# A hand-ordered opening of the first feed-forward stage, with kept normed tiles and another order of its first gate products

## The chip, the cores and the metric

The kernel runs on one core of a Trainium2 chip. The metric is the device time of one execution in microseconds (us), the median of several runs. The engines are PE (TensorE, matrix products), DVE (VectorE), ACT (ScalarE), POOL (GpSimd) and SP (SyncE, which here issues the loads and stores). PEld is the loading of weights into PE, beside PE's products.

## What is computed

The reference is a decoder layer of width 1024 over 1024 tokens with 16 meta tokens in front of them, 1040 columns in all. A gated feed-forward half step comes first, then two attention branches, then a second feed-forward half step and a last norm. Only the opening of the first feed-forward step is touched here:

```python
def rmsnorm(x, g):
    xf = x.astype(jnp.float32)
    y = xf * lax.rsqrt(jnp.mean(xf * xf, axis=-1, keepdims=True) + EPS)
    return (y * g.astype(jnp.float32)).astype(x.dtype)

def swiglu(x, w_gate, w_up, w_down):
    return (jax.nn.silu(x @ w_gate) * (x @ w_up)) @ w_down

h = h + 0.5 * swiglu(rmsnorm(h, norm_ffn1[l]), w_ffn1_gate[l], w_ffn1_up[l], w_ffn1_down[l])
```

The hidden width is 2816, that is 22 blocks of 128 columns.

## The kernel before

**Layout.** The activations lie transposed: eight tiles (k = 0 to 7) of 128 channels each, with the tokens as columns, in two halves x = 0 (528 columns, the meta tokens first) and x = 1 (512 columns). A product in float32 quality is made of three float16 products (`mm3`, lines 144 to 147): every weight and every activation is split into a high part, written by ACT, and the rest, written by DVE (here called the low part). A float32 weight piece of 128 x 1024 is loaded by SP (`load_raw`, line 126), its high part is made on L130 (ACT) and its low part on L131 (DVE).

**The norm of a half.** `square_into` (L157, L160, L161) squares each tile on ACT and adds up on DVE. For the second half POOL does both (L617, L619). `norm_stats` sums over the channels with PE (L171, one column for each block of 128 tokens), then takes the mean on DVE (L173), the root on ACT (L175), the reciprocal on DVE (L176), and makes one step of Newton's method in four small DVE instructions (L178 to L181). `norm_bcast` (L191) spreads the result over 128 partitions with PE, into PSUM. `norm_u` then makes for each k the normed tile "un" on DVE (L219, with the spread factor read from PSUM), its high part on ACT (L221) and its low part on DVE (L222). For the combined blocks below the spread factor is also kept in SBUF (rb, L224).

**The first pair.** `plain_pair(0)` (line 266) makes the first two gate blocks and the first two up blocks by plain products, one half and one piece of weights after the other (`proj`). The gate's result goes through Silu on ACT (L278), and is multiplied by the up result on DVE (L283). Between the halves the weights of the first combined job are made (`wide_weights`) and `make_t` is called.

**The combined jobs.** All other blocks go by a scheme of seven products in place of eight (a Strassen-like scheme over pairs of blocks). It needs four sums of activations t1 to t4. `make_t` computes the normed tiles a second time on DVE (`gained`, L302, from h, the gain and rb; four tiles that `norm_u` kept in `saved` are taken over), combines them on POOL (`combine`, L289 to L292, four subtractions for each of four i), and splits the results into "tb" tiles (`split_x`, L235 on ACT, L236 on DVE). `fast` (line 415) then emits the seven products (L327), one after the other, and after each of them lets `pump` emit a share of the side work that waits in `todo`: splits of hidden tiles (L540, L541), sums and splits of the next job's weights (L390 to L395, L341, L344). After that comes the reader of the product. Of the seven products p1 and c11 share the bank "pa": c11 adds onto p1, so c11 can only begin when ACT has copied p1 out ("base", L451). The order of a gate or up job is `UP` (line 434): p1, p6, p7, p5, c11, p74, p53. Here p6 reads t2, p7 reads t3, p5 reads t1, p74 reads t4, and p1, c11 and p53 read only plain activations.

**What sets the order.** In the combined jobs PE, DVE, ACT and POOL run exactly in the order in which the code emits their instructions (`tc.manual_schedule(engines=ORDERED)`, line 545); an instruction that waits holds up all that stand behind it on its engine. The opening, up to the end of `plain_pair`, is put in order by the framework's own scheduler. SP issues the loads in one queue: eight tiles of the first half, the unit matrix, the gains, two weight pieces, then eight tiles of the second half (L114); later pieces follow as buffers come free.

Of the kernel before, what the change touches and what calls it, by code (L numbers as in the profile page):

```python
# [9 lines left out]
F16 = mybir.dt.float16  # L10
# [4 lines left out]
ALU = mybir.AluOpType  # L15
# [40 lines left out]
def layer_kernel(ctx: ExitStack, tc: tile.TileContext, xT, gains, wgu1, wd1, win, wvi, wbs, wbw, wout,  # L56
# [52 lines left out]

    h = [[hp([P, HW[x]], F32, "h") for _ in range(KD)] for x in range(2)]  # L110

    def load_h(x):
        for k in range(KD):
            nc.sync.dma_start(h[x][k], xT[k][:, HS0[x]:HS0[x + 1]])  # L114

    load_h(0)
    ident = cst.tile([P, P], F32, name="ident")
    nc.sync.dma_start(ident, eye)
    g_all = cst.tile([P, 4, KD], F32, name="g_all")
# [43 lines left out]
    def new_acc():  # L163
        return big.tile([P, 528], F32, tag="acc", name="acc", bufs=2)

    def norm_stats(acc, subs):
        bl = blocks_of(subs)
        nb = len(bl)
        ps = trps("nsum")
        for j, (b0, _) in enumerate(bl):  # L170
            nc.tensor.matmul(ps[:, j:j + 1], acc[:, b0:b0 + P], ones, start=True, stop=True)  # L171
        a = small(8, "n_a")
        nc.vector.tensor_scalar(a[:, :nb], ps[:, :nb], 1.0 / D, EPS, op0=ALU.mult, op1=ALU.add)  # L173
        r = small(8, "n_r")
# [3 lines left out]
        nc.vector.tensor_mul(e[:, :nb], r[:, :nb], r[:, :nb])  # L178
        nc.vector.tensor_mul(e[:, :nb], e[:, :nb], a[:, :nb])
        nc.vector.tensor_scalar(e[:, :nb], e[:, :nb], -0.5, 1.5, op0=ALU.mult, op1=ALU.add)  # L180
        nc.vector.tensor_mul(r[:, :nb], r[:, :nb], e[:, :nb])  # L181
        return r

    def norm_bcast(r, subs):
        bl = blocks_of(subs)
# [41 lines left out]
    def ffn(u, rb, hs, gi, wgu, wd, other_half, passes, saved):  # L227
# [187 lines left out]
        def fast(weights, blocks, order):  # L415
            a11, a12, s2, s3, s1, s4, a22 = weights
            b11, b21, b22, t1, t2, t3, t4 = blocks
            what = {"p1": ("pa", a11, b11, wa, wa, True), "p6": ("pb", s2, t2, wa, wa, True),
                    "p7": ("pc", s3, t3, wb, wb, True), "p5": ("pd", s1, t1, wb, wb, True),
                    "c11": ("pa", a12, b21, wa, wa, False), "p74": ("pc", a22, t4, wa, wa, False),  # L420
                    "p53": ("pd", s4, b22, wb, wb, False)}
# [24 lines left out]
        def half_products(m, blocks, first, done):  # L446
            make = fbtmp if m else ftmp
            for what, ps in joint(blocks, UP):
# [3 lines left out]
                elif what == "p6":  # L452
                    nc.vector.tensor_add(va(base), ps, va(base))
                elif what == "c11":
                    first(ps)
                elif what == "p7":
                    c22 = make("c22")
                    nc.vector.tensor_add(vb(c22), ps, va(base)[:, :, :wb])  # L458
                elif what == "p5":
                    nc.vector.tensor_add(vb(c22), ps, vb(c22))  # L460
                    done(3, c22, vb(c22))
                elif what == "p74":
                    c21 = make("c21")
                    nc.vector.tensor_add(va(c21), ps, va(base))
                    done(2, c21, va(c21))
                else:
                    c12 = va(base)[:, :, :wb]
                    nc.vector.tensor_add(c12, ps, c12)
                    done(1, base, c12)

        def gate_part(blocks):
            gates = [None] * 4
# [70 lines left out]
        vals = plain_pair(0)  # L543
        blocks = (u[0][:4], u[0][4:], u[1][4:]) + tuple(t_blocks)
        with tc.manual_schedule(engines=ORDERED):
            for f0, f1 in F_GROUPS:
# [4 lines left out]
                for f in range(f0, f1, 2):  # L551
# [14 lines left out]
                        for i, t in ((0, spare), (2, vals[1]), (1, vals[0]), (3, vals[2])):  # L566
                            split_later(down[3 + i], t, i % 2 ^ 1, tail)
                    if f < NF - 2:
                        gates = gate_part(blocks)
# [27 lines left out]
            ready = acc, subs, done  # L597
        return acc

    u1, rb1 = [], []  # L600

    def ffn1_norm(x):
        acc = new_acc() if x == 0 else acc_b
        for k in range(KD if x == 0 else 0):
            square_into(k, h[x][k], acc)
        u, rb = norm_u(norm_stats(acc, SUB_ALL[x]), h[x], 0, SUB_ALL[x], keep=True, saved=saved1 if x else None)
        u1.append(u)
        rb1.append(rb)

    saved1 = {}  # L610
    raws = [load_raw(wgu1[i], 1024) for i in range(2)]
    load_h(1)
    ffn1_norm(0)
    acc_b = new_acc()
    for k in range(KD):
        sq = acc_b if k == 0 else ftmp("sq")
        nc.gpsimd.tensor_mul(sq[:, :512], h[1][k], h[1][k])  # L617
        if k:
            nc.gpsimd.tensor_add(acc_b[:, :512], acc_b[:, :512], sq[:, :512])  # L619
    u2 = []  # L620
    hsp = dram.tile([KD, P, T], F32, name="hspill")

    def mix_norm(x, r):
        u2.append(norm_u(r, h[x], 1, SUB_ALL[x]))
        for k in range(KD):
            nc.sync.dma_start(hsp[k][:, HS0[x]:HS0[x + 1]], h[x][k])

    acc = ffn(u1, rb1, h, 0, wgu1, wd1, lambda: ffn1_norm(1),
              ((0, SUB_ALL[0], lambda r: mix_norm(0, r)), (1, SUB_ALL[1], None)), saved1)
    close_phase()  # L630
    open_phase("mix")

# [569 lines left out]
```

## Time and profile before

| what | value |
|---|---|
| median of 3 runs | 2032.15 us (2031.77 to 2035.65) |
| profiled execution, its time | 2033.16 us |
| span of that execution in the profile | 2031.1 us |
| mean granted clock of PE, as a share of full speed | 0.988 |
| PE busy over the span | 1936.5 us, 95% |
| DVE busy over the span | 1627.2 us, 80% |
| ACT, POOL busy over the span | 901.0 us, 44%; 386.9 us, 19% |

The profile is of one execution: its own time lies 2.1 us above its span, and 1.0 us above the median. All stretches below are in microseconds from the span's start.

### The profile page before, as it was taken

To read this page: it belongs to the slowest core of one execution; us is meant where nothing else is said; L and a number is where in the kernel's file an instruction comes from. 1 tells how busy PE (TensorE), PEld (TensorE's weight loads), DVE (VectorE), ACT (ScalarE), POOL (GpSimd) and SP (SyncE) were. 2 spreads that over 40 slices of the span, in tenths; PEclk is the share of its full clock that TensorE was granted. 3 is DMA by queue.
4 is the path that set the end of the run, shared out by engine and by line. 5 is a ranking of instruction groups with operands and counts; after the bars stand their busy time and mean duration, and the time that the engine had idled before them with its cause. 6 is when DMAs were issued, how large, how long until landed. Compare 5 with 4: busy or idle time off the path is not lost.

```text
span 2031.1 us, 32839 instructions
## 1 busy us (share of the span) xinstructions
PE 1936.5 (95%) x13080; PEld 1197.3 (59%) x13080; DVE 1627.2 (80%) x2779; ACT 901.0 (44%) x1602; POOL 386.9 (19%) x313
## 2 busy tenths in 40 slices
PE   5899999999999989899999999998899999999997
PEld 4588888888888556454545654444344444444443
DVE  7888788778875799999999964566987787788767
ACT  4433233333323446589885643433433243233232
POOL 3611312221310132221001000002322212312200
PEclk9999999999999999999999999999999999999998
DMA  4011111111113543212020024241112121111213
GB/s 158 11 63 48 58 63 50 55 64 58 48 63 105 183 141 112 99 59 73 17 63 17 27 68 156 78 164 49 34 55 68 48 72 47 63 62 47 76 38 130
DMA packets 58873, 146.95 MB, mean 72 GB/s; under 512 B 7264, under 2 KB 13408, under 8 KB 58720
## 3 DMA queue, kind: packets, MB, share of 16 engines
q1 hardware_dynamic: 58720, 144.86, 22.3%
q8 instruction: 102, 1.67, 0.3%
q14 instruction: 51, 0.42, 0.1%
HBM read 130.01 MB, written 14.76 MB: 71 GB/s over the span
## 4 chain that ended last, share of the span: by engine, by line
PE 70%; DVE 18%; ACT 4%; issue 4%; DMA 2%; POOL 2%; DVEq 0%; SPq 0%; ACTq 0%; POOLq 0%
PE pc L327 14%; PE pd L327 14%; PE pa L327 14%; PE pb L327 7%; PE p_br L999 2%; DVE sc L791 2%; DVE u L222 2%; DVE wsp L131 1%; PE p_gate L147 1%; PE p_gate L145 1%; PE p_gate L146 1%; DVE m L790 1%; PE p_out L146 1%; PE p_out L147 1%; PE p_out L145 1%
## 5 line engine op out<-in xcount | busy, mean ns | idle before, releaser
L327 PEld LDWEIGHTS <-wsp 128*128 128x128 f16 x4176 | 410.0, 98 | 214.2 <-issue 12.3
L327 PEld LDWEIGHTS <-x 128*128 128x128 f16 x3132 | 307.3, 98 | 157.9 <-issue 8.5
L327 PE MATMUL pa<-u,wsp 128*128 128x264 f16 (+1 forms) x1440 | 224.7, 310 | 0.0
L131 DVE SCALAR_TENSOR_TENSOR wsp<-wst,wsp 128x1024 f16<-128x1024 f32 (+2 forms) x130 | 134.8, 1038 | 54.6 <-ACT wsp L130 54.3
L130 ACT ACTIVATE wsp<-wst 128x1024 f16<-128x1024 f32 (+2 forms) x130 | 111.7, 863 | 140.1 <-PE p_out L147 45.9
L147 PEld LDWEIGHTS <-wsp 128*128 128x128 f16 x912 | 90.5, 99 | 94.5 <-issue 12.3
L145 PEld LDWEIGHTS <-wsp 128*128 128x128 f16 x912 | 91.0, 100 | 85.1 <-issue 4.1
L146 PEld LDWEIGHTS <-wsp 128*128 128x128 f16 x912 | 90.7, 99 | 80.2 <-issue 3.9
L327 PE MATMUL pb<-tb,wsp 128*128 128x264 f16 (+1 forms) x720 | 113.7, 312 | 8.1 <-ACT tb L235 5.5
L327 PE MATMUL pc<-tb,x 128*128 128x264 f16 (+1 forms) x720 | 113.9, 313 | 6.6 <-DVE c L458 6.4
L327 PE MATMUL pc<-tb,wsp 128*128 128x256 f16 (+1 forms) x720 | 114.2, 314 | 0.0
L327 PE MATMUL pd<-tb,x 128*128 128x256 f16 (+1 forms) x720 | 110.7, 308 | 0.0
L327 PE MATMUL pd<-u,x 128*128 128x256 f16 (+1 forms) x720 | 110.7, 308 | 0.0
L289 POOL TENSOR_TENSOR t<-g,g 128x512 f32<-128x512 f32 x16 | 25.5, 1595 | 436.0 <-DVE g L494 436.0
L812 ACT ACTIVATE jk<-sc,s5nb 128x784 f16<-128x784 f32 (+2 forms) x93 | 97.9, 1052 | 19.0 <-DVE s5nb L827 15.3
L341 ACT ACTIVATE wsp<-sa 128x1024 f16<-128x1024 f32 (+1 forms) x62 | 60.2, 971 | 103.4 <-DVE sa L393 103.4
L327 PE MATMUL pa<-hid,wsp 128*128 128x264 f16 (+1 forms) x648 | 103.1, 310 | 0.0
L341 ACT ACTIVATE wsp<-wst 128x1024 f16<-128x1024 f32 (+1 forms) x62 | 59.9, 967 | 94.3 <-DMA wst<-in_wgu_dram 49.9
L327 PE MATMUL pd<-hid,x 128*128 128x256 f16 (+1 forms) x648 | 101.6, 308 | 0.0
L147 PE MATMUL p_gate<-u,wsp 128*128 128x512 f16 x256 | 97.0, 379 | 1.4 <-DVE wsp L131 1.4
L145 PE MATMUL p_gate<-u,wsp 128*128 128x512 f16 x256 | 97.0, 379 | 0.0
L146 PE MATMUL p_gate<-u,wsp 128*128 128x512 f16 x256 | 97.0, 379 | 0.0
(234 smaller groups left out, 4147.6 us busy)
## 6 DMA issues: line engine op xcount, KB each, us to landing
wst<-in_wgu_dram SPq DMA_DIRECT2D x88, 512.0 KB, 3.7
wst<-in_win_dram SPq DMA_DIRECT2D x44, 512.0 KB, 3.5
wst<-in_wd_dram SPq DMA_DIRECT2D x48, 384.0 KB, 3.4
wst<-in_wd_dram SPq DMA_DIRECT2D x32, 256.0 KB, 2.7
wst<-in_wout_dram SPq DMA_DIRECT2D x16, 512.0 KB, 4.1
qscr<-ry SPq DMA_DIRECT2D x20, 256.0 KB, 2.1
q<-qscr SPq DMA_DIRECT2D x20, 256.0 KB, 3.0
wst<-in_wbs_dram SPq DMA_DIRECT2D x16, 256.0 KB, 2.7
```

What stands on the lines that cost most here:

```text
L130: nc.scalar.activation(sp[:, 0, :n], st[:, :n], AF.Copy, scale=WS)
L131: nc.vector.scalar_tensor_tensor(sp[:, 1, :n], st[:, :n], WS, sp[:, 0, :n], op0=ALU.mult, op1=ALU.subtract)
L145: nc.tensor.matmul(ps, w[:, 0, wcols], xt[:, 0, xcols], start=start, stop=False)
L146: nc.tensor.matmul(ps, w[:, 0, wcols], xt[:, 1, xcols], start=False, stop=False)
L147: nc.tensor.matmul(ps, w[:, 1, wcols], xt[:, 0, xcols], start=False, stop=stop)
L222: nc.vector.tensor_sub(u[k][:, 1, s0:s1], t[:, :w], u[k][:, 0, s0:s1])
L289: nc.gpsimd.tensor_sub(vb(t1), vb(b1), va(a1)[:, :, :wb])
L327: nc.tensor.matmul(ps[:, s, :n], w[:, a, wc], tiles[k][:, y, s * stride:s * stride + n], start=start and k == 0 and j == 0, stop=stop and ...
L341: nc.scalar.activation(sp[:, 0, :n], st[:, :n], AF.Copy, scale=WS)
L791: nc.vector.match_replace(out=raw, in_to_replace=m8, in_values=raw, imm_value=MARK)
L812: nc.scalar.activation(junk[:, :w], sc[b][0], AF.Sign, bias=bias[:, j:j + 1], accum_out=s[:, j:j + 1])
L999: nc.tensor.matmul(pb, bw[:, a, c * P:(c + 1) * P], oT[:, y, c, :], start=c == 0 and n == 0, stop=c == 3 and n == 2)
```

## The change

The loads of the first half are cut at column 272: first eight loads of 272 columns, then the unit matrix, the gains and weight pieces 0, 1 and 2, then eight loads of the other 256 columns, then piece 3, then the second half. The pieces 2 and 3 go to other buffers ("wS"), so that they need not wait for the first two.

`first_pair` takes the place of `plain_pair(0)`, of the two norms before it, of `wide_weights` and of `make_t`, in the first stage alone. It handles the tokens in three slices (272, 256 and 512 columns), and its instructions on PE, DVE, ACT and POOL run in the order written. For each slice and each k the three steps "un", high, low are emitted one behind the other, and then the products of that k with the four weight pieces. The eight "un" tiles of each half are kept in full, and POOL combines these; nothing is computed twice. The squares of all slices are on ACT and DVE. The first slice's spread factor is read from PSUM, those of the other two are first copied to SBUF by ACT. The first gate job runs in the order `FIRST`, where c12 is made from a seventh product p3 = s4 b22 in a bank of its own in place of p53 added onto p5. Newton's step takes three DVE instructions in place of four in every norm of the kernel. The second feed-forward step keeps `plain_pair` and `gate_part`.

```diff
-    load_h(0)
+    CUT = 272
+    for k in range(KD):
+        nc.sync.dma_start(h[0][k][:, :CUT], xT[k][:, :CUT])
...
+    def newton(r, e, a):
+        nc.vector.scalar_tensor_tensor(e, r, -0.5, r, op0=ALU.mult, op1=ALU.mult)
+        nc.vector.tensor_mul(e, e, a)
+        nc.vector.scalar_tensor_tensor(r, e, 1.5, r, op0=ALU.add, op1=ALU.mult)
...
+                    "p53": ("pd", s4, b22, wb, wb, False), "p3": ("pb", s4, b22, wb, wb, True)}
...
+        def first_products(m, blocks, first, done):
+            for what, ps in joint(blocks, FIRST):
+                if what == "p1":
+                    base = fbtmp("base")
+                    nc.scalar.activation(va(base), ps, AF.Copy)
+                elif what == "p3":
+                    c12 = ftmp("c12")
+                    nc.scalar.activation(vb(c12), ps, AF.Copy)
+                elif what == "c11":
+                    first(ps)
+                elif what == "p7":
+                    c22 = ftmp("c22")
+                    nc.vector.tensor_add(vb(c22), ps, va(base)[:, :, :wb])
+                elif what == "p5":
+                    nc.vector.tensor_add(vb(c22), ps, vb(c22))
+                    nc.vector.tensor_add(vb(c12), ps, vb(c12))
+                elif what == "p6":
+                    nc.vector.tensor_add(vb(c22), ps[:, :, :wb], vb(c22))
+                    done(3, c22, vb(c22))
+                    nc.vector.tensor_add(va(base), ps, va(base))
+                    nc.vector.tensor_add(vb(c12), va(base)[:, :, :wb], vb(c12))
+                    done(1, c12, vb(c12))
+                else:
+                    c21 = ftmp("c21")
+                    nc.vector.tensor_add(va(c21), ps, va(base))
+                    done(2, c21, va(c21))
...
+            for k in range(KD):
+                sq(0, k)
+                if k:
+                    add(0, k)
+            stats(0, W[0][:, 1, :])
+            whi(0)
+            root(0)
+            rb[0] = spread(0, W[1][:, 1, :], False)
+            un_(0, 0), uhi(0, 0), ulo(0, 0)
+            wlo(0), whi(1)
+            mm(0, 0, 0)
...
+            stats(1, W[0][:, 1, :])
+            un_(0, 7), uhi(0, 7), ulo(0, 7)
+            root(1)
+            for i in range(4):
+                mm(0, i, 7)
+            rb[1] = spread(1, W[3][:, 1, :], True)
+            for k in range(KD):
+                un_(1, k), uhi(1, k), ulo(1, k)
+                for i in range(4):
+                    mm(1, i, k)
+                if k == 1:
+                    silu(0, 0), silu(0, 1)
+                    times(0, 0), times(0, 1)
+                    sq(2, 0), sq(2, 1)
+                if k == 2:
+                    warm = small(1, "n_warm")
+                    nc.scalar.activation(warm, a_[1][:, 0:1], AF.Sqrt)
+                if k > 1 and k < 5:
+                    sq(2, 2 * k - 2), sq(2, 2 * k - 1) if k < 5 else None
+                    add(2, 2 * k - 3), add(2, 2 * k - 2)
+                if k == 5:
+                    add(2, 7)
+                    stats(2, W[0][:, 0, :])
+                if k == 6:
+                    root(2)
+                    rb[2] = spread(2, W[1][:, 0, :], True)
+            tb = [[None] * 4 for _ in range(4)]
+            order = (0, 4, 1, 5, 2, 6, 3, 7)
+            src = {}
+            for n, k in enumerate(order):
+                un_(2, k), uhi(2, k), ulo(2, k)
+                if n == 0:
+                    silu(1, 0), silu(1, 1)
+                if n == 2:
+                    times(1, 0), times(1, 1)
+                if n < 6:
+                    for i in range(4):
+                        mm(2, i, k)
+            for i in range(4):
+                for k in order[6:]:
+                    mm(2, i, k)
+            for i in range(4):
+                t1 = ftmp("t1")
+                combine(un[0][i], un[1][i], un[0][i + 4], un[1][i + 4], t1)
...
+            for x1, half in ((x1a, lo), (x1b, hi)):
+                high(x1, r1[:, half], 512), low(x1, r1[:, half], 512)
+            v.tensor_add(sb[:, lo], r2[:, lo], r2[:, hi])
+            v.tensor_sub(sa[:, lo], sb[:, lo], r1[:, lo])
+            split(0, 0), split(2, 0)
+            v.tensor_sub(sa[:, hi], r1[:, lo], r2[:, lo])
+            v.tensor_sub(sb[:, hi], r1[:, hi], sa[:, lo])
+            silu(2, 0), silu(2, 1)
+            high(x3, sb, 1024), low(x3, sb, 1024)
+            split(1, 0), split(3, 0)
+            split(0, 1), split(2, 1)
+            times(2, 0), times(2, 1)
+            high(x2, sa, 1024), low(x2, sa, 1024)
+            split(1, 1)
+            high(x4, r2[:, hi], 512), low(x4, r2[:, hi], 512)
+            for j in (0, 2, 1):
+                split(j, 2)
+            for j in (2, 0, 1):
+                split(j, 3)
+            for i in (1, 2, 3):
+                split(3, i)
+            fetch(1)
+            return vals, u, tb
...
+        FIRST = ("p1", "p3", "c11", "p7", "p5", "p6", "p74")
...
-    load_h(1)
+    for i in (2, 3):
+        raws.append(ph["sb"].tile([P, 1024], F32, tag="wS", name="wst", bufs=2))
+    nc.sync.dma_start(raws[2], wgu1[2])
     for k in range(KD):
-        sq = acc_b if k == 0 else ftmp("sq")
-        nc.gpsimd.tensor_mul(sq[:, :512], h[1][k], h[1][k])
-        if k:
-            nc.gpsimd.tensor_add(acc_b[:, :512], acc_b[:, :512], sq[:, :512])
+        nc.sync.dma_start(h[0][k][:, CUT:], xT[k][:, CUT:HS0[1]])
+    nc.sync.dma_start(raws[3], wgu1[3])
+    for k in range(KD):
+        nc.sync.dma_start(h[1][k], xT[k][:, HS0[1]:])
```

In the diff `sq`, `uhi`, `whi`, `silu` and `high` end in one ACT instruction each, `add`, `ulo`, `wlo`, `times`, `low` and `un_` in one DVE instruction each; `split(j, i)` is one of ACT and one of DVE, and `mm(s, i, k)` is three matmuls of slice s with weight piece i. The scratch tiles `ftmp` ("rb" of slices 1 and 2, the last four "tu", and "t1") share six buffers.

## Rows read from the trace of the kernel before

**Rows 1.** Windows: from:to, length, busy PE, PEld, DVE, ACT, POOL, clock, DMA share, GB/s

```profile
0.00:20.18 20.18, 4.80 (x20) 4.45 (x21) 10.55 (x18) 10.29 (x15) 7.20 (x10) 1.00 0.78 273
20.18:84.71 64.53, 51.71 (x304) 32.74 (x304) 60.95 (x85) 29.54 (x50) 31.83 (x22) 0.95 0.14 48
...
114.80:214.80 100.00, 100.00 (x903) 88.07 (x901) 80.22 (x103) 36.52 (x55) 19.54 (x12) 1.00 0.18 54
```

**Rows 2.** Timeline of PE: start, us, instruction, [idle before it <- what ended that]

```profile
20.18 0.38 PE L145 MATMUL pg<-u,wsp 128*128 128x264 f16 x1 [0.20 <-ACT u L221]
...
68.31 0.38 PE L146 MATMUL pg<-u,wsp 128*128 128x512 f16 x1 [0.19 <-DVE u L222]
...
84.71 2.86 PE L327 MATMUL pa<-u,wsp 128*128 128x264 f16 x24
...
107.85 4.49 PE L327 MATMUL pc<-tb,x 128*128 128x264 f16 x24 [3.58 <-DVE c L458]
...
114.80 2.86 PE L327 MATMUL pa<-u,wsp 128*128 128x264 f16 x24
117.50 2.86 PE L327 MATMUL pb<-tb,wsp 128*128 128x264 f16 x24
```

**Rows 3.** Groups of DVE, first 100 us: count | busy us, mean ns | idle before

```profile
L222 DVE TENSOR_TENSOR u<-un,u 128x272 f16<-128x272 f32 (+2 forms) x24 | 21.1, 903 | 0.2
...
L302 DVE SCALAR_TENSOR_TENSOR tu<-h,g_all,rb 128x528 f32<-128x528 f32 (+1 forms) x12 | 10.7, 925 | 0.0
```

**Rows 4.** Timeline of SP: the first eight loads are issued

```profile
0.74 3.71 SPq L114 DMA_DIRECT2D h<-in_xT_dram  x8
```

**Rows 5.** Timeline of DVE in the opening

```profile
6.46 4.77 DVE L161 TENSOR_TENSOR acc<-acc,sq 128x528 f32<-128x528 f32 x6 [0.67 <-ACT sq L160]
...
15.31 1.12 DVE L180 TENSOR_SCALAR n_e<-n_e 128x5 f32<-128x5 f32 x1
...
35.32 1.21 DVE L131 SCALAR_TENSOR_TENSOR wsp<-wst,wsp 128x1024 f16<-128x1024 f32 x1
...
38.53 0.48 DVE L219 SCALAR_TENSOR_TENSOR un<-h,g_all,nbc 128x256 f32<-128x256 f32 x1
38.93 0.42 DVE L222 TENSOR_TENSOR u<-un,u 128x256 f16<-128x256 f32 x1
...
50.68 0.17 DVE L180 TENSOR_SCALAR n_e<-n_e 128x4 f32<-128x4 f32 x1
...
61.29 4.44 DVE L222 TENSOR_TENSOR u<-un,u 128x512 f16<-128x512 f32 x3
65.65 1.39 DVE L219 SCALAR_TENSOR_TENSOR un<-h,g_all,nbc 128x512 f32<-128x512 f32 x2
...
68.78 0.68 DVE L236 TENSOR_TENSOR tb<-t,tb 128x512 f16<-128x512 f32 x1
...
77.26 3.14 DVE L302 SCALAR_TENSOR_TENSOR tu<-h,g_all,rb 128x528 f32<-128x528 f32 x3
```

**Rows 6.** Timeline of ACT in the opening

```profile
3.75 0.64 ACT L157 ACTIVATE acc<-h 128x528 f32<-128x528 f32 x1 [1.74 <-DMA h<-in_xT_dram]
...
39.05 0.42 ACT L221 ACTIVATE u<-un 128x256 f16<-128x256 f32 x1 [0.62 <-DVE un L219]
...
72.65 1.28 ACT L278 ACT_TABLE_LOAD   x1
...
97.74 0.59 ACT L451 ACTIVATE base<-pa 128x528 f32<-128x528 f32 x1
```

**Rows 7.** Timeline of PE: sums and spreading of the norm

```profile
11.29 2.29 PE L171 MATMUL nsum<-ones,acc 128*128 128x1 f32 x10 [11.29 <-DVE acc L161]
...
51.20 2.05 PE L191 MATMUL nbc<-ident,n_r 128*128 128x128 f32 x8 [3.72 <-DVE n_r L181]
```

**Rows 8.** Windows, columns as in rows 1: one with eight POOL instructions, one after a wait

```profile
53.35:68.78 15.43, 12.11 (x71) 7.51 (x70) 15.43 (x17) 9.39 (x17) 12.53 (x8) 0.89 0.00 1
107.85:112.00 4.15, 4.15 (x23) 3.02 (x23) 2.86 (x4) 1.77 (x4) 0.00 (x0) 0.59 0.45 159
```

More of the change, by code (lines that the diff above doesn't have):

```diff
@@ L110, in layer_kernel @@
     h = [[hp([P, HW[x]], F32, "h") for _ in range(KD)] for x in range(2)]
-    def load_h(x):
-        for k in range(KD):
-            nc.sync.dma_start(h[x][k], xT[k][:, HS0[x]:HS0[x + 1]])
-    load_h(0)
+    CUT = 272
+    for k in range(KD):
+        nc.sync.dma_start(h[0][k][:, :CUT], xT[k][:, :CUT])
     ident = cst.tile([P, P], F32, name="ident")
@@ L177, in norm_stats @@
         e = small(8, "n_e")
[L178 to L181, printed above, removed]
-        return r
+        newton(r[:, :nb], e[:, :nb], a[:, :nb])
+        return r
+    def newton(r, e, a):
+        nc.vector.scalar_tensor_tensor(e, r, -0.5, r, op0=ALU.mult, op1=ALU.mult)
+        nc.vector.tensor_mul(e, e, a)
+        nc.vector.scalar_tensor_tensor(r, e, 1.5, r, op0=ALU.add, op1=ALU.mult)
     def norm_bcast(r, subs):
@@ new lines, in first_gate, with first, done @@
+        def first_gate(blocks):
+            gates = [None] * 4
+            def first(ps):
+                t = ftmp("g11")
+                nc.scalar.activation(va(t), ps, AF.Silu, scale=1.0 / WS)
+                gates[0] = (t, va(t))
+            def done(i, t, v):
+                nc.scalar.activation(v, v, AF.Silu, scale=1.0 / WS)
+                gates[i] = (t, v)
+            first_products(0, blocks, first, done)
+            return gates
+        FIRST = ("p1", "p3", "c11", "p7", "p5", "p6", "p74")
@@ L544, in ffn @@
+        if u is None:
+            with tc.manual_schedule(engines=ORDERED):
+                vals, u, t_blocks = first_pair()
+            parts = [first_gate]
+        else:
+            vals = plain_pair(0)
+            parts = [gate_part]
         blocks = (u[0][:4], u[0][4:], u[1][4:]) + tuple(t_blocks)
@@ L568, in ffn @@
                     if f < NF - 2:
-                        gates = gate_part(blocks)
+                        gates = (parts.pop() if parts else gate_part)(blocks)
                 if not last:
@@ L598, in ffn @@
         return acc
[L600 to L610, printed above, removed]
     raws = [load_raw(wgu1[i], 1024) for i in range(2)]
-    load_h(1)
-    ffn1_norm(0)
-    acc_b = new_acc()
+    for i in (2, 3):
+        raws.append(ph["sb"].tile([P, 1024], F32, tag="wS", name="wst", bufs=2))
+    nc.sync.dma_start(raws[2], wgu1[2])
     for k in range(KD):
-        sq = acc_b if k == 0 else ftmp("sq")
-        nc.gpsimd.tensor_mul(sq[:, :512], h[1][k], h[1][k])
-        if k:
-            nc.gpsimd.tensor_add(acc_b[:, :512], acc_b[:, :512], sq[:, :512])
+        nc.sync.dma_start(h[0][k][:, CUT:], xT[k][:, CUT:HS0[1]])
+    nc.sync.dma_start(raws[3], wgu1[3])
+    for k in range(KD):
+        nc.sync.dma_start(h[1][k], xT[k][:, HS0[1]:])
     u2 = []
@@ L626, in mix_norm @@
             nc.sync.dma_start(hsp[k][:, HS0[x]:HS0[x + 1]], h[x][k])
-    acc = ffn(u1, rb1, h, 0, wgu1, wd1, lambda: ffn1_norm(1),
-              ((0, SUB_ALL[0], lambda r: mix_norm(0, r)), (1, SUB_ALL[1], None)), saved1)
+    acc = ffn(None, None, h, 0, wgu1, wd1, None,
+              ((0, SUB_ALL[0], lambda r: mix_norm(0, r)), (1, SUB_ALL[1], None)), None)
     close_phase()
```

123 lines of the change are left out of this document (121 added, 2 removed).

## The prediction

> **What bounds the kernel now.** I read the windows first. From 114.80 us on PE is busy all the time at a granted clock of 1.00 [rows 1]; before that it is not: 51.7 of the 64.5 us of the first pair. So what the opening gains or loses goes through to the end, and the number to forecast is the start of the first up job's first product, now 114.80 [rows 2]. Then the timeline of PE: first weight product at 20.18, pair done at 84.71, a wait of 3.58 us for DVE at 107.85. Then DVE: it is busy for 60.95 of the 64.53 us of the pair [rows 1]. DVE bounds the opening, with what slows it. The groups show two things the change takes away: 10.7 us for computing twelve normed tiles again, and low parts that mean 903 ns [rows 3], though one of 256 columns takes 0.42 and one of 512 0.68 [rows 5]. The slow ones stand beside POOL: three of 512 columns in 4.44 us, 1.48 each.
>
> Records of DVE overlap by some 0.08 us (a 0.48 starts 0.40 ahead of the next [rows 5]). So I count 0.40 and 0.37 for 256 to 272 columns, 0.61 for 512, 1.15 for a 1024-column weight low part (1.21); on ACT 0.40, and 0.56 for 512 (0.59 for 528 [rows 6]). A product on PE takes 2.70 at full clock (114.80 to 117.50 [rows 2]), one of 256 columns 2.62, by its columns.
>
> **Part by part.** I follow DVE in the written order, and let it wait wherever that order makes it.
>
> *To the first product.* The eight first loads are issued 0.46 us apart (3.71 for eight [rows 4]). The first square begins at 3.75 [rows 6], so the eighth tile is there at 7.0, and the last add ends at 7.9; now it ends at 11.23 [rows 5]. The block sums take 6 of the 10 matmuls of 2.29 us, 1.4; the spreading 6 at 2.05/8, 1.5 [rows 7]. Between them lie mean, root, reciprocal and three steps, 1.2 with their hand-overs: one small step takes 0.17 without POOL and took 1.12 beside it [rows 5], and POOL no longer squares. DVE begins the first normed tile at 12.3, PE its first product at 13.2, 7.0 us earlier.
>
> *Slices 0 and 1: what the written order costs.* Normed tile, high part and low part of one k follow each other, so DVE waits for ACT each time: 0.40 + 0.5 (ACT's 0.42 [rows 6] and two hand-overs) + 0.40 = 1.3 us. Slice 0: eight of them 10.4, four weight low parts 4.6, seven adds for slice 1 2.6, its mean and root 1.0, a wait for PE's sums of 1.1; together 19.7, to 32.0. Then PE spreads, ACT copies: 2.0. Slice 1: eight steps 10.4, seven adds for slice 2 4.3 (on POOL before), two products 0.8, mean and root 1.0, and four waits. The Silu table is loaded (1.28 [rows 6]) and used ahead of the third high part: 1.3. The root's table and a square stand ahead of the next: 1.1. The mean of slice 2 waits for the twelve matmuls of k = 5 and the sums: 2.0. ACT's copy of the third factor waits for k = 6 and the spreading (2.05 [rows 7]), and the last low part behind it: 3.1. Sum 24.0; slice 2 begins at 58.0.
>
> *Slice 2.* 0.61 + 0.7 + 0.61 eight times, 15.4, and two products 0.8. POOL's sixteen subtractions begin here and run 1.57 us each (12.53 for eight [rows 8]) to 1.7, some 26.5 us, to 85.5. Beside POOL a low part takes 1.48 for 0.68 and a product with both inputs in SBUF 1.05 (3.14 for three), while two reading PSUM at 65.65 take 0.69 each [rows 5]. Five low parts add 3.8, six normed tiles 2.4, since their factor now lies in SBUF. Sum 22.4, DVE at 80.4. PE needs 0.216 a matmul (76 from 68.31 to 84.71 [rows 2]), 20.7 for 96, so it ends 4.5 us behind DVE's last low part: 84.9, as now.
>
> The Trainium skill, GPSIMD Engine Reference, section Key points, says that GpSimd shares its SBUF interfaces with VectorE and contends with instructions that have two SBUF inputs. By that rule copying the factor to SBUF is what exposes the normed tiles of slice 2; with PSUM the sum would be 2.4 us shorter. The trace agrees (1.05 against 0.69).
>
> *First gate job.* c11, the third product, waits for ACT's copy of p1, and ACT comes to that copy only behind all sixteen high parts of the combined tiles. DVE does eight instructions up to the weight sum that the third weight tile needs: 8 x 0.61, and 2.7 more while POOL runs, to 88.0. ACT then makes that weight high part, 0.97, fourteen high parts of 0.56, two more of weights 1.5, three of hidden tiles 1.7, and the copy, 0.6: 12.4, to 100.4. From there PE is free of waits: c11 2.70, p7 and p5 2.62 each, p6 and p74 2.70 each, and 1.8 for a low clock behind the wait, as at 107.85, where a product of 2.70 took 4.49 [rows 2] at a granted 0.59, partly the 1.2 GHz level [rows 8]. That makes 15.1: the first up product begins at 115.5, 0.7 us later than now.
>
> *At no cost.* Loads: the first product's weights are issued a few loads later, but are needed only 6 us on; the first tile halves, second tiles and four pieces come to 6.5 MB; at 273 GB/s [rows 1] that is 24 us, and the second half is squared from 38 on. The loads for the first up job start behind the last weight low part at 96 and are wanted at 101; if late they hold ACT, then c12's copy, not c11. The up job's second weight tile is ready at about 115, and wanted at 118. The two extra adds (1.2 us) and one copy of the new order lie beside products. Newton's step is one instruction of 0.17 shorter in eight norms; some are covered, so I take 0.3 us off.
>
> **Sum.** +0.7 - 0.3 = +0.4. The profiled execution (2033.16, span 2031.1) lies 1.0 above the median; I set the difference on the median: 2032.6. A measurement of this kernel can tell some 0.2%, 4 us; so this is no change.
>
> **Rivals.** *Faster: less contention.* If the sixteen subtractions slow DVE by half of what rows 5 and 8 give, slice 2 and the eight instructions end 4.5 us earlier, ACT's copy too: 2028. With none at all PE alone ends the pair by 80.5 and the copy is at 92, for 2025; that is the low end. For it: POOL may wait for tiles and so run beside fewer instructions. Against it: POOL was busy 12.5 of 15.4 us at 53 to 69 and every low part there was slow.
>
> *Slower: POOL's chain becomes the end.* Six scratch buffers carry two factors, four normed tiles and four results of POOL. If POOL's first result gets the buffer of slice 2's factor, it waits for the last normed tile, at about 75 with nothing beside it, and sixteen steps end at 101; ACT's last high part and the copy at 104, c11 behind them. That is +4.5: 2037. It decides whether POOL's first subtraction starts before or behind slice 2's last normed tile. Against it: the first factor's buffer is free earlier.
>
> *Slower: PE stays at the low clock through slices 0 and 1*, since it gets short bursts. A k then costs twelve matmuls at twice 2.70/24, 2.7 us of PE, and passes DVE's step; up to 6 us: 2038. For it: low clock behind a wait at 107.85 [rows 8]; against it: the mean of 0.95 over the present pair, with its many gaps [rows 1].
>
> *The change does nothing* because another engine holds the opening is inside the forecast: the start gained, 7.0, is spent on waits in slice 1.
>
> **How the numbers follow.** Forecast 0.45 (its own range 2028.5 to 2036.5), faster rival 0.28, the slower ones 0.15 and 0.12. Chances: faster 0.28, same 0.45, slower 0.27. The range takes in the faster rival's end and both slower ones with 2 us for my waits: 2025 to 2040.
>
> **What would show it.** First weight product near 13; no second computing of tiles; DVE in slice 1 with gaps of 1 to 3 us at the two table loads, the mean and the third factor; slice 2 beginning near 58; PE waiting at c11 for ACT until near 100; first up product near 115.5. I am wrong if slice 1 takes under 18 us, if low parts beside POOL take under 1 us, or if c11 waits for nothing.

## The result and the profile after

The changed kernel takes 2050.84 us (median of 4 runs, 2049.3 to 2051.44), the kernel before 2033.76 in its 4 runs: a ratio of 1.0083, 95% interval 1.0065 to 1.01. That is slower by 17 us, or 0.8%; the whole interval lies above 1, and the time lies outside the range. The profiled execution took 2049.3 us, with a span of 2047.5.

Windows of after, cut at the same events as [rows 1] (columns as there):

```profile
13.67:86.75 73.08, 55.91 (x312) 33.02 (x312) 46.09 (x82) 30.52 (x60) 11.90 (x8) 0.98 0.16 55
86.75:129.31 42.56, 24.99 (x170) 18.84 (x168) 40.33 (x43) 18.65 (x31) 21.42 (x13) 0.80 0.14 50
129.31:229.31 100.00, 100.00 (x903) 88.07 (x901) 81.60 (x105) 37.13 (x56) 19.64 (x12) 1.00 0.18 54
```

PE is full from the first up product on, as before. So the question is again how late that product is. Timeline of PE in after, against [rows 2]:

```profile
13.67 0.39 PE L143 MATMUL pw<-u,wsp 128*128 128x272 f16 x1 [1.05 <-ACT u L645]
...
29.03 0.43 PE L143 MATMUL pw<-u,wsp 128*128 128x272 f16 x1
29.26 0.32 PE L144 MATMUL pw<-u,wsp 128*128 128x272 f16 x1
29.41 0.28 PE L145 MATMUL pw<-u,wsp 128*128 128x272 f16 x1
29.52 0.28 PE L143 MATMUL pw<-u,wsp 128*128 128x272 f16 x1
...
86.75 2.86 PE L327 MATMUL pa<-u,x 128*128 128x264 f16 x24
97.09 1.04 PE L327 MATMUL pb<-u,x 128*128 128x256 f16 x4 [7.48 <-ACT x L341]
99.45 4.45 PE L327 MATMUL pb<-u,x 128*128 128x256 f16 x20 [1.32 <-DVE x L344]
108.02 4.42 PE L327 MATMUL pa<-u,x 128*128 128x264 f16 x24 [4.12 <-ACT base L475]
112.27 2.78 PE L327 MATMUL pc<-tb,wsp 128*128 128x256 f16 x24
...
125.02 4.45 PE L327 MATMUL pc<-tb,x 128*128 128x264 f16 x24 [4.65 <-DVE c L483]
129.31 2.86 PE L327 MATMUL pa<-u,wsp 128*128 128x264 f16 x24
```

The products p1, p3, c11, p7, p74 and the first up product stand at 86.75, 97.09, 108.02, 112.27, 125.02 and 129.31. The last was at 114.80 before and forecast for 115.5. The first weight product is at 13.67, 0.5 us behind the forecast of 13.2. So the opening won 6.5 us at its head, and everything behind that head lost 21. Timeline of DVE in after (L640 makes the normed tile, L649 the low part; L344, L767 to L771 and L236 are weights and combined tiles; L483 reads the result of p7):

```profile
20.92 0.50 DVE L640 SCALAR_TENSOR_TENSOR tu<-h,g_all,pw 128x272 f32<-128x272 f32 x1 [1.86 <-PE pw L145]
21.91 0.44 DVE L649 TENSOR_TENSOR u<-tu,u 128x272 f16<-128x272 f32 x1 [0.49 <-ACT u L645]
23.73 0.50 DVE L640 SCALAR_TENSOR_TENSOR tu<-h,g_all,pw 128x272 f32<-128x272 f32 x1 [1.38 <-PE pw L145]
...
38.47 0.48 DVE L640 SCALAR_TENSOR_TENSOR tu<-h,g_all,rb 128x256 f32<-128x256 f32 x1 [1.72 <-ACT rb L628]
...
62.18 0.75 DVE L640 SCALAR_TENSOR_TENSOR tu<-h,g_all,rb 128x512 f32<-128x512 f32 x1
...
82.31 3.44 DVE L344 SCALAR_TENSOR_TENSOR x<-wst,x 128x512 f16<-128x512 f32 x2
85.67 1.79 DVE L767 TENSOR_TENSOR sb<-wst 128x512 f32<-128x512 f32 x1
87.50 1.67 DVE L768 TENSOR_TENSOR sa<-sb,wst 128x512 f32<-128x512 f32 x1
89.09 1.78 DVE L236 TENSOR_TENSOR tb<-t,tb 128x512 f16<-128x512 f32 x1
...
94.16 1.78 DVE L771 TENSOR_TENSOR sb<-wst,sa 128x512 f32<-128x512 f32 x1
...
123.68 0.68 DVE L344 SCALAR_TENSOR_TENSOR x<-wst,x 128x512 f16<-128x512 f32 x1
124.29 0.68 DVE L483 TENSOR_TENSOR c<-pc,base 128x512 f32<-128x512 f32 x1
```

Slice 1 begins at 38.47, slice 2 at 62.18 and ends at 82.3. The eight instructions behind it take 13.6 us. Much later, p7 is done near 115 (112.27 and 2.78), but DVE reads it only at 124.29, behind side work of the next job such as L344. The eight instructions stand beside POOL, whose timeline in after reads:

```profile
68.78 1.63 POOL L292 TENSOR_TENSOR tu<-tu 128x528 f32<-128x528 f32 x1
80.57 1.27 POOL L289 TENSOR_TENSOR t<-tu 128x512 f32<-128x512 f32 x1 [10.15 <-DVE tu L640]
...
90.28 1.70 POOL L291 TENSOR_TENSOR tu<-tu,t 128x512 f32<-128x512 f32 x1
```

POOL stands still for 10 us until slice 2's last normed tile is made, then runs beside those eight instructions. ACT's split of the third weight tile of the gate job waits for the last of them (timeline of ACT in after):

```profile
95.98 1.06 ACT L341 ACTIVATE x<-sb 128x1024 f16<-128x1024 f32 x1 [9.66 <-DVE sb L771]
...
107.38 0.59 ACT L475 ACTIVATE base<-pa 128x528 f32<-128x528 f32 x1
```

A second loss lies far behind. The last output product of the second half's merge (p_out) starts at 1381.94 before and at 1399.08 after, 17.1 us later; up to the first down product (637.28, then 651.79) the difference is 14.5. PE has a wait of 3.27 us at 1360.61, for ACT's tile mt; before, the longest wait of p_out in that stretch is 0.35.

### The profile page after: what moved, and what is told of

Read it like the earlier page. It is cut to its first block, busy times and chain, and to the rows that moved or that the text cites. A ratio compares the mean times of both kernels' runs of the same rounds, so it can differ in the third digit from the quotient of the medians.

```text
span 2047.5 us, 32859 instructions
## 1 busy us (share of the span) xinstructions
PE 1940.7 (95%) x13080; PEld 1195.7 (58%) x13080; DVE 1619.9 (79%) x2783; ACT 905.6 (44%) x1623; POOL 369.9 (18%) x298
## 3 DMA queue, kind: packets, MB, share of 16 engines
q1 hardware_dynamic: 59872, 144.87, 22.4%
q8 instruction: 102, 1.67, 0.3%
## 4 chain that ended last, share of the span: by engine, by line
PE 70%; DVE 18%; ACT 5%; issue 3%; DMA 2%; POOL 1%; SPq 0%; DVEq 0%; ACTq 0%; POOLq 0%
PE pc L327 14%; PE pd L327 14%; PE pa L327 14%; PE pb L327 7%; PE p_br L1256 2%; DVE sc L1048 2%; PE p_gate L143 1%; PE p_gate L145 1%; PE p_gate L144 1%; PE p_out L144 1%; PE p_out L145 1%; DVE wsp L129 1%; PE p_out L143 1%; DVE m L1047 1%; ACT jk L1069 1%
## 5 line engine op out<-in xcount | busy, mean ns | idle before, releaser
L327 PEld LDWEIGHTS <-x 128*128 128x128 f16 x3180 | 313.6, 99 | 175.7 <-issue 13.9
L327 PE MATMUL pa<-u,wsp 128*128 128x264 f16 (+1 forms) x1392 | 218.9, 312 | 0.0
L129 DVE SCALAR_TENSOR_TENSOR wsp<-wst,wsp 128x1024 f16<-128x1024 f32 (+2 forms) x125 | 125.1, 1002 | 58.3 <-ACT wsp L128 58.1
L128 ACT ACTIVATE wsp<-wst 128x1024 f16<-128x1024 f32 (+2 forms) x125 | 106.6, 856 | 143.4 <-PE p_out L145 41.8
L289 POOL TENSOR_TENSOR t<-g,g 128x512 f32<-128x512 f32 x15 | 23.7, 1578 | 403.3 <-DVE g L521 403.3
```

Source lines behind the costliest of these rows:

```text
L128: nc.scalar.activation(sp[:, 0, :n], st[:, :n], AF.Copy, scale=WS)
L129: nc.vector.scalar_tensor_tensor(sp[:, 1, :n], st[:, :n], WS, sp[:, 0, :n], op0=ALU.mult, op1=ALU.subtract)
L289: nc.gpsimd.tensor_sub(vb(t1), vb(b1), va(a1)[:, :, :wb])
L327: nc.tensor.matmul(ps[:, s, :n], w[:, a, wc], tiles[k][:, y, s * stride:s * stride + n], start=start and k == 0 and j == 0, stop=stop and ...
```

## The experiments

The theory: the opening is late by waits that follow from the written order and from shared tiles, and by DVE standing beside POOL. The rivals: POOL's chain, or the new order of the gate job. The first column of times is the median; "first up" is the start of the first up product in the profile. Ratios are to the kernel before, run beside it (its pooled medians 2033.5 to 2034.3).

| kernel | time | ratio, interval | first up |
|---|---|---|---|
| after | 2050.84 | 1.0083, 1.0065 to 1.01 | 129.31 |
| e1_own_factor | 2046.15 | 1.0057, 1.0039 to 1.0075 | 125.62 |
| e2_old_newton | 2048.41 | 1.0073, 1.0058 to 1.0088 | 129.58 |
| e3_subs_on_dve | 2043.61 | 1.0044, 1.0027 to 1.0061 | 123.94 |
| e4_old_gate_order | 2049.88 | 1.0077, 1.0062 to 1.0092 | 128.68 |
| e5_bank_pairs | 2047.17 | 1.0071, 1.0055 to 1.0087 | 124.45 |
| e6_reader_first | 2050.28 | 1.0086, 1.007 to 1.0101 | 126.08 |
| e7_next_tile_first | 2040.19 | 1.0032, 1.0019 to 1.0044 | 119.69 |
| e11_banks_and_next_tile | 2036.07 | 1.0005, 0.9997 to 1.0014 | 114.58 |
| e8_all | 2026.66 | 0.9968, 0.9956 to 0.9981 | 108.63 |
| e9_side_work_order | 2027.54 | 0.9971, 0.9962 to 0.9981 | 100.09 |
| e10_sums_in_waits | 2027.03 | 0.9968, 0.9955 to 0.998 | 105.34 |
| e12_new_newton_alone | 2035.45 | 1.0005, 0.9996 to 1.0013 | 113.80 |

**POOL's chain.** The third slice's factor gets a buffer of its own, so that POOL's results need not wait for it:

```diff
-                    t = ftmp("rb")[:, :c1 - c0]
+                    t = (ntmp if s == 2 else ftmp)("rb")[:, :c1 - c0]
```

> The changed kernel, with the spread factor of slice 2 in a buffer of its own, so that the second scratch tile of POOL's subtractions need not wait for slice 2's last normed tile. In the changed kernel POOL stands still from 70.4 to 80.6 us for it and ends its sixteen subtractions at 100.5. Theory 'late scratch': that wait is the loss. POOL then ends near 90, ACT's copy of p1 comes near 100 in place of 108, the first up product starts near 119 in place of 129.3, and the time falls by about 10 us to 2040. Rival 'contention stays': POOL's subtractions cost DVE their own length wherever they lie, so slice 2 gets longer by what the weights' sums get shorter; the first up product starts at 127 to 129, the time stays at 2048 to 2051.

The 10 us stall went, and POOL ended at 91.8. But c11 stayed at 108.15 (108.02 in after): POOL's chain was not the end. What POOL no longer did beside the eight instructions it did beside slice 2, where normed tiles now take 1.75 (timeline of DVE in e1):

```profile
74.75 1.75 DVE L640 SCALAR_TENSOR_TENSOR tu<-h,g_all,rb 128x512 f32<-128x512 f32 x1
...
92.26 0.68 DVE L767 TENSOR_TENSOR sb<-wst 128x512 f32<-128x512 f32 x1
```

The 3.7 us that the first up product won came behind c11: p74's wait fell from 4.65 to 2.34, and its product ran in 2.86 in place of 4.45. The median is 4.7 us below that of after, with intervals that overlap. The rival was right about what happens (slice 2 takes 6.3 us more, the eight instructions 6.5 less), though its 127 to 129 was too late.

**Contention itself.** The same, and the sixteen subtractions moved from POOL to DVE, two in each step of slice 2:

```diff
-                un_(2, k), uhi(2, k), ulo(2, k)
+                un_(2, k), uhi(2, k)
+                for _ in range(2):
+                    if pend:
+                        pend.pop(0)()
+                ulo(2, k)
```

> As the run with the factor's own buffer, and the sixteen subtractions are done by DVE instead of POOL, two in each step of slice 2 between the normed tile and its low part, where DVE waits 0.7 us for ACT. Theory 'contention': beside POOL each DVE instruction with two SBUF inputs lasts as long as POOL's own, 1.7 us for 0.61. Without POOL slice 2 takes about 20 us, the eight instructions after it 5 in place of 13, ACT's copy of p1 comes near 101, and the first up product starts near 116: the time falls by 12 to 13 us to about 2038. Rival 'DVE is full': sixteen more instructions on the bounding engine cost 16 x 0.61 = 10 us and give back what the contention cost; the first up product starts at 125 or later, 2046 or more.

The instructions that took 1.67 to 1.79 in after take 0.64 to 0.69 here (timeline of DVE in e3):

```profile
89.38 1.28 DVE L344 SCALAR_TENSOR_TENSOR x<-wst,x 128x512 f16<-128x512 f32 x2
90.58 0.68 DVE L782 TENSOR_TENSOR sb<-wst 128x512 f32<-128x512 f32 x1
```

Although DVE now makes sixteen more instructions of 0.68 to 0.71, the first up product comes 1.7 us earlier than in e1. So by the profile POOL's help cost DVE a little more than the work it took over. The theory's 116 and 2038 were missed by 8 and 6 us; the result lies nearer the rival's 125 and 2046, since the sixteen instructions give back most of what the contention cost. The medians of e1 and e3 lie 2.5 us apart the same way, with intervals that overlap.

**The order of the gate job.** One word, `first_gate` to `gate_part`.

> The changed kernel with the first gate job in the order of the other jobs (p1, p6, p7, p5, c11, p74, p53). Theory 'order': c11 as third product waits for ACT (4.1 us) and p74 as last waits for DVE's reader of p7 (4.65 us), each with a low clock behind it; with the old order c11 comes fifth and both waits go, but p6 waits for the combined tiles t2, ready at 111: the first up product starts at 126 to 130, a gain of at most 3 us. Rival 'order helps': the new order hides work while the combined tiles are late, and the old one starts the up product at 131 or later, 2052 or more.

The first up product came 0.6 us earlier; PE's wait of 10.46 us then stood at p6, the second product, for ACT's high part of a weight. The new order is not the cause, and in this kernel it is worth nothing that the medians show.

**Tiles shared in PSUM.** The factor of slice 0 and the sums of the norm lay in the other half of a two-bank tile that running products write. Four pieces of one slice are paired instead, so that those halves are idle:

```diff
-            bank = lambda i, s: W[i][:, s % 2, :sl[s][2] - sl[s][1]]
+            bank = lambda i, s: W[2 * (s % 2) + i // 2][:, i % 2, :sl[s][2] - sl[s][1]]
...
-            rb[0] = spread(0, W[1][:, 1, :], False)
+            rb[0] = spread(0, W[3][:, 1, :], False)
```

> The changed kernel with the eight PSUM banks of the opening paired otherwise: a pair holds two pieces of one slice, not one piece of two slices, and the first factor lies in a pair that PE writes only in slice 1. Theory 'shared pair': in slice 0 DVE's normed tiles for k = 3 and 4 waited 1.86 and 1.38 us for PE, because the factor they read lay in the same pair of banks as a sum that PE was writing; without that slice 2 starts 3 us earlier (59 in place of 62.2), the first up product at 126 to 127, the time falls by 2.5 to 3.5 us to about 2047.5. Rival 'low clock': PE, which took 0.22 us a matmul until 29.3, bounds slice 0 itself; DVE's waits only move, slice 2 starts at 61.5 or later, 2049 or more.

DVE's two waits for `pw` (1.86 and 1.38 in after) are gone. From the first normed tile (13.19) to slice 1's first tile (34.95) it is 21.8 us, where after takes 25.8. Slice 2 begins at 57.36 in place of 62.18 (timeline of DVE in e5):

```profile
34.95 0.48 DVE L640 SCALAR_TENSOR_TENSOR tu<-h,g_all,rb 128x256 f32<-128x256 f32 x1 [1.73 <-ACT rb L628]
...
57.36 0.75 DVE L640 SCALAR_TENSOR_TENSOR tu<-h,g_all,rb 128x512 f32<-128x512 f32 x1
```

All of that arrives at the first up product: 124.45, 4.9 us earlier. The median is 3.7 us lower, with intervals that overlap.

**The reader of a product ahead of the side work**, in the first gate job:

```diff
-                pump(share)
+                if "p3" not in order:
+                    pump(share)
                 yield name, ps[:, :, :n]
+                if "p3" in order:
+                    pump(share)
```

> The changed kernel, in whose first gate job the reader of each product is emitted ahead of the side work that goes with it, not behind. Theory 'reader behind side work': in the changed kernel ACT's copy of p1 stands behind three high parts of hidden tiles (1.7 us) and DVE's reader of p7 behind two weight low parts; p74, which adds onto p7's bank, waits 4.65 us for it, with a low clock behind (1.8 us). With the reader first c11 starts near 106.3 in place of 108.0, p74's wait is 2.5 us or less, and the first up product starts near 124: 2045 to 2047. Rival 'DVE is late anyway': the reader of p7 still stands behind all low parts of the combined tiles; the side work is only pushed back and the up job waits for its weights: 2049 or more.

c11's wait fell from 4.12 to 2.53 and p74's from 4.65 to 3.12 in the profile, but the median is that of after within its interval, and the profiled execution (2045.43) lies 4.9 us below that median; by itself this is unproven.

**The next normed tile ahead of the low part**, so that DVE has work while ACT makes the high part:

```diff
+                if k != ks[-1]:
+                    un_(s, ks[ks.index(k) + 1])
                 nc.vector.tensor_sub(u[x][k][:, 1, c0:c1], un[x][k][:, c0:c1], u[x][k][:, 0, c0:c1])
```

> The changed kernel, in which DVE makes the normed tile of the next k ahead of the low part of this one, in all three slices, so that it need not stand still while ACT makes the high part. Theory 'waits of the written order': DVE waits 0.48 to 0.70 us for ACT at each of 24 steps, 12.8 us in all; slices 0 and 1 shorten by 6 to 8 us, slice 2 starts at 54 to 56 in place of 62.2, the first up product at 121 to 124, and the time falls to 2042 to 2045. Rival 'PE and ACT set the pace': slice 0 goes by PE's low clock, slice 1 by ACT's table loads and the mean on PE; then the wait only changes its place, slice 2 starts at 60 or later, 2048 or more.

The largest single effect: 9.6 us at the first up product. DVE's waits up to 135 us, first in after, then in e7 (us in total, times, longest):

```profile
DVE u L649 <- ACT u L645: 16.4, 24, 3.5
...
DVE tu L640 <- PE pw L145: 3.2, 2, 1.9
```

```profile
DVE tu L645 <- PE pw L145: 4.2, 3, 1.9
DVE u L657 <- ACT u L650: 4.1, 5, 2.6
```

24 waits became 5. The waits for the shared tile grew instead, since DVE now runs further ahead of PE.

**Do the two add up?** After with these two edits alone:

> The changed kernel with two of the single repairs only: the four pieces of a slice paired by bank so that no factor shares a tile with a running product, and the next normed tile written ahead of each low part. Theory (both are waits of the written order, at different places): their effects in the opening, 4.9 and 9.6 us, add up; the first up product begins at about 115, as before the change, and the time is 2034 to 2037. Rival (both shorten the same wait): no better than the second alone, first up product at 119 to 120, 2039 to 2041.

```profile
114.58 2.86 PE L327 MATMUL pa<-u,wsp 128*128 128x264 f16 x24
```

14.7 us earlier than after, where the two effects sum to 14.5 (timeline of PE in e11). They add up, and the loss of the opening is undone by removing two kinds of wait: the time is that of before within its interval.

**All six together** (e1, e2, e3, e5, e6, e7):

> All of these together: four-instruction Newton step outside the opening, the factor of slice 2 in a buffer of its own, the sixteen subtractions on DVE in slice 2, the banks paired by slice, the reader first, the next normed tile first. Theory 'sum of waits': about 3 us from the banks, 4 from the next tile first in slices 0 and 1 beyond that, 5 from the subtractions, 4 from the reader, 2.5 from the Newton order: the first up product starts at 112 to 116 and the time is 2030 to 2035, at or a little below the kernel before. Rival 'DVE's own work': DVE is the bound whatever the order, and its busy time up to the up job hardly falls; the first up product starts at 120 or later, 2038 or more.

This beats both kernels: 7.2 us below the median of before, 24 below after. The single effects on the median of e2, e3, e5, e6 and e7 (e3 contains e1) sum to 24.5; each of them is uncertain by some 3 us, so that the sum fits this closely is in part luck. What is left is p74's wait (timeline of PE in e8, and its window from slice 2's end to the first up product, columns as in [rows 1]):

```profile
94.34 2.86 PE L330 MATMUL pb<-tb,wsp 128*128 128x264 f16 x24
103.72 5.08 PE L330 MATMUL pc<-tb,x 128*128 128x264 f16 x24 [6.51 <-DVE c L489]
```

```profile
69.70:108.60 38.90, 27.82 (x189) 20.07 (x189) 36.60 (x50) 21.44 (x36) 7.91 (x4) 0.87 0.15 50
```

DVE is busy for 36.6 of those 38.9 us. So either the order of its work holds p74, or its sum does.

**Order or sum.** In the kernel of all six, the side work of the first gate job in another order, none of it ahead of p7:

```diff
-                if "p3" in order:
-                    pump(share)
+                if "p3" in order and name not in ("p1", "p3", "c11"):
+                    pump(1.75 * share)
...
+            if "p3" in order:
+                todo[:] = own[:10] + own[10:] + todo + tail
```

> The kernel with all six repairs, and the side work of the first gate job in another order: the weights of the next job come ahead of the hidden tiles, and none of it is issued before the seventh product's operands are there. Theory (DVE's reader of c22a stands behind side work, and that alone holds p74): p74 loses its wait of 6.51 us, the first up product begins at about 102 in place of 108.6, and the time is 2019 to 2023. Rival (DVE is full there, 36.6 of 38.9 us, so the same work only moves): PE waits later, in the up job, and the time stays at 2025 to 2028.

Timeline of PE in e9:

```profile
97.39 2.86 PE L330 MATMUL pc<-tb,x 128*128 128x264 f16 x24
100.09 2.86 PE L330 MATMUL pa<-u,wsp 128*128 128x264 f16 x24
...
112.15 4.45 PE L330 MATMUL pd<-tb,x 128*128 128x256 f16 x24 [3.88 <-DVE c L504]
```

The wait was there because p74's bank was read by an instruction queued behind side work: it is gone. But the work moved into the up job, and PE waits there. Of 8.5 us at the first up product, 1.95 are left at the first down product (631.11, then 629.16), and the time is not shorter. The rival is right: DVE is full there, in e9 still for 36.7 of the 39.9 us from 100.09 on. So a wait that is gone at the first up product is not yet time that is won.

**Sums moved into slice 1's waits:**

> The kernel before this one in the list, and one low part and the four weight sums of the first gate job moved ahead into DVE's waits in slice 1. Theory (DVE bounds slice 2 and the gate job, while slice 1 has gaps of 1 to 3 us): slice 2 begins within 1 us of where it did, five instructions of about 0.6 us leave the stretch behind it, and the time is 3 us shorter. Rival (the loads of those weights come too late for slice 1, or the waits there are ended by DVE's own chain): slice 2 begins 3 us later, and nothing is gained or some is lost.

Slice 2 begins at 54.74 in place of 51.12, and nothing is gained: the rival again, by its numbers. Some 1.1 of these 3.6 us are there before the first moved instruction, which nothing here explains; another 1.1 come with the moved low part, which waits 2.24 us for ACT's high part (DVE at 33.19), and slice 1 gets 1.4 longer.

**Newton's step.** The four old instructions in after, then the three new ones alone in the kernel before:

> The changed kernel with the four-instruction Newton step in the norms outside the new opening. From the first up product to the end of the attention part both kernels run alike, but in the last product stage before the second feed-forward step the changed kernel loses some 3 us more: PE waits 3.27 us for ACT at 1360. Theory 'new order': the shorter step made the framework's scheduler put that stage's instructions in another order; with the old step the order of before returns, the up product stays at 129.3 and the time falls by 2 to 3 us, to 2048. Rival 'late start': the later opening itself shifts loads there; then nothing changes, 2050 to 2051.

> The kernel before the change with nothing but its shorter step of Newton. Theory (one instruction less in each norm leads to another order of the instructions in the second half's merge and output products, and PE waits there): the opening within 0.5 us of before, about 2.4 us lost in the stretch from 1345 us on, time 2035 to 2037. Rival (what was lost there came with the late opening and not with the step): 2032 to 2034, no new wait of PE behind 1345.

Waits of PE from 1290 to 1420 us in e12, and in after:

```profile
PE p_out L145 <- ACT mt L1070: 3.1, 1, 3.1
```

```profile
PE p_out L143 <- ACT mt L1328: 3.3, 1, 3.3
```

Both kernels with the new step have this wait; in before and in e2, with the old step, the longest of p_out there is 0.35. That stage is put in order by the framework, and the instructions of DVE and ACT stand in another order in e12 than in before: counted from the first up product, ACT makes this mt 2.4 us later (1344.06 less 114.80, then 1345.49 less 113.80). In the timed medians the effect is 2.4 us in one pair (intervals that overlap) and within the interval in the other, so its size stays open. From the first down product to the last p_out, the five traces with the old step in the later norms (before, e2, e8, e9, e10) take 744.4 to 746.8 us, and the nine with the new one 746.8 to 751.1, in the mean 3.6 more. In e1, e5 and e11 this stretch is longest, 750.0 to 751.1, more than that one wait explains. That is why the last p_out starts in e1 at 1399.17, as in after (1399.08), though the first up product came 3.7 earlier.

## Why the prediction was wrong

The reading of the profile held for before and after: of the 17.1 us at p_out, 14.5 are there at the first up product, and 2.6 more are lost behind it. It does not hold for every change: in the profiles of e1 (an execution 2.9 us above its median) and e9, most of what is won at that product is lost behind it. The steps, by their own terms:

| step | forecast | measured | difference |
|---|---|---|---|
| first normed tile | 12.3 | 12.66 | +0.4 |
| slice 0, to slice 1's first tile | 21.7 | 25.8 | +4.1 |
| slice 1 | 24.0 | 23.7 | -0.3 |
| slice 2 | 22.4 | 20.1 | -2.3 |
| eight instructions | 7.6 | 13.6 | +6.0 |
| ACT's chain to c11 | 12.4 | 12.0 | -0.4 |
| c11 to the first up product | 15.1 | 21.3 | +6.2 |

The differences sum to 13.7, of 13.8 (129.31 less 115.5). ACT's chain was added up 0.2 too low: its own terms give 12.6.

*Slices 0 and 1* was right on the written order: a step of 1.3 us, 24 waits, slice 1 within 0.3 us. It did not see that those waits were the largest thing to repair (e7). They are in its sum, though: of the two things that e11 repairs, only the shared tile was missing from the forecast. What failed is slice 0: it let the factor be read at no cost, while the factor lies in a tile that products write. Two waits, together 3.2 us, are in the trace; e5 takes them away, and slice 0 then takes 21.8, as forecast. They end where PE's products end, and PE is behind: up to 29.26 a product of 272 columns takes 0.227 us, the pace of the 1.2 GHz level. The third rival, low clock in slices 0 and 1, was so half right: the low pace held for most of slice 0, and in slice 1 only from 56.84 to 59.60 (granted clock 0.50; 0.93 over the slice). The low pace alone was not the loss: in e5 it lasts up to 24.4, and slice 0 is on time.

*Slice 2 and the eight instructions* mis-sized and misplaced the contention. I spread it over five low parts and six normed tiles (6.2 us) and 2.7 us behind. POOL stood still for 10 us of slice 2, as the rival on POOL's chain had it, but with its second scratch tile and not its first, and then met all eight: 6 us too little there, 2.3 too much in slice 2. I took 1.05 to 1.48 us for one instruction beside POOL; it is 1.7. In e3, without POOL, the eight take 5.0. The rival's condition came true in that form, its price did not: with the stall gone, c11 did not move (e1). Its 2037 was 14 us short. The Trainium skill's rule in GPSIMD Engine Reference, section Key points (contention with instructions that have two SBUF inputs), is borne out by e1: normed tiles with the factor in SBUF take 1.75 beside POOL, those with it in PSUM took 0.69 [rows 5]. What it costs is in this case's rows alone.

*First gate job* failed in one sentence: "From there PE is free of waits". The prediction counts operands and no reader of a bank. p7's result is read by an instruction queued on DVE behind side work, at a cost of 4.65 us and a slow product behind it (4.45 in place of 2.86). Set against e8, e9 shows this by taking the wait away. How much of these 6.2 us is the order and how much is DVE's work stays open, since in e9 the time did not follow. c11's wait for ACT's copy was foreseen, and ACT's chain has its length; it begins 8 us later. *At no cost* held for the loads: the one that was late made ACT wait 2.88 us at 111.80, behind that copy.

*Newton* was counted at -0.3. In e12's profile it wins 1.0 in the opening, and brings a wait of 3.1 us in a stage that the framework orders. The prediction does not ask what a shorter instruction list does to a planner elsewhere.

The range was too narrow for a simple reason: three terms of 4 to 6 us each had the same sign, each rival was priced by itself, and p74's wait stood in none.

## What to carry to other kernels

When an order is written out by hand, check for every wait three queues, not one: the operands, the bank or buffer (who read it last, and what stands ahead of that reader), and the tile that a dependency is tracked on. Write the next independent instruction ahead of each one that waits for another engine, before other things are tuned: here that was the largest single gain. And where two engines slow each other, count on the time of both, and ask which instructions will meet, not how many.

## What was not expected of the hardware

**DVE beside POOL.** A 512-column instruction with two inputs in SBUF takes 0.68 on the record alone (e3) and 1.67 to 1.79 beside POOL (after), and POOL's goes from 1.27 to between 1.61 and 1.74. They advance as a pair, one pair in about 1.70 us (89.09, 90.79, 92.46, 94.16 are the starts). Alone, one after the other, they would take 0.61 and 1.27, or 1.88, an estimate from these rows. So the two overlap by about 0.2 us only. The Trainium skill, Trainium Architecture — The Big Picture, section What this means for kernel authors, calls the port that DVE and GpSimd share an exclusive lock, not a split of bandwidth; by that rule the pair would take that estimate of 1.88, and the trace comes near it with 1.70, though not quite to it.

**PE's first 29 us.** In after, products of 272 columns start 0.227 us apart up to 29.26 and 0.115 apart behind, so they change from the 1.2 to the 2.4 GHz level there. The granted clock from 13.67 to 29.26 is given as 1.00 all the same. In e5 the change comes at 24.4, in e11 at 21.1. The kernel before has it too; its timeline of PE shows 264 columns in 0.22 us, and the column says 1.00 there as well:

```profile
28.78 0.43 PE L146 MATMUL pu<-u,wsp 128*128 128x264 f16 x1
29.00 0.43 PE L147 MATMUL pu<-u,wsp 128*128 128x264 f16 x1
29.22 0.32 PE L145 MATMUL pu<-u,wsp 128*128 128x264 f16 x1
...
29.59 0.27 PE L147 MATMUL pg<-u,wsp 128*128 128x264 f16 x1
29.70 0.27 PE L145 MATMUL pg<-u,wsp 128*128 128x264 f16 x1
```

So the mean of 0.95 that the prediction set against its low-clock rival was read from a column that gives 1.00 for the first 9 us of that pair, at half the pace of what follows. At the head of a profile the pace of the products has to be read, not the clock's column.
